# Attention in runs of a head pair, and its product with v by heads

## The chip, the cores and the metric

The kernel runs on one core of one Trainium2 chip. The metric is the device time of one execution in microseconds; the time before is the median of three runs. A profiled execution gives the trace from which all durations come.

## The reference

A two-layer encoder over 512 tokens of width 1024 (an 8 x 64 grid). Each layer is a half-step gated FFN, a mixer, and a second half-step FFN; the change lies in the attention of the mixer.

```
def mixer(h, w_in, gate_bias, rpb, w_na_out, w_f_out, w_o):
    z = h @ w_in                        # q, k, v (512 columns each), uf, ga, gf
    y_na = neighbourhood_attention(q, k, v, rpb) @ w_na_out
    y_f = fourier_mix(uf) @ w_f_out
    return (sigmoid(ga + gate_bias[0]) * y_na + sigmoid(gf + gate_bias[1]) * y_f) @ w_o

# attention, 8 heads of 64: blocks of 16 columns x 8 rows = 128 queries,
# each against a band of 32 columns x 8 rows = 256 keys
    s = einsum('brjqhd,brjuvhd->brjhquv', qg, k_win) * scale + bias      # masked to a 16-column window
    p = softmax(s)
    o = einsum('brjhquv,brjuvhd->brjqhd', p, v_win)
```

Everything is float32, and the kernel keeps that accuracy on TensorE by splitting each operand into a high part (rounded by ScalarE to the fp32r format) and a low part (the rest, by VectorE). A product is then three matmuls: high by high, high by low, low by high (`mm3`, lines 291 to 294).

## The kernel before, in words

Tokens are permuted so that 128 neighbouring positions are one block of queries j (0 to 3) and the 256 keys of a block are two consecutive pieces of 128 positions. The mixer (`stage_mixer`) first projects u and v with tokens on partitions: `proj_V` leaves four tiles of v (tag "v": high half, low half), and three DMA pairs build shifted tiles "vs" that straddle two of them, so that `vch` holds seven tiles of 128 keys. Then come the Fourier products (`four_pos`, `four_ch`) and, by head pair hp (heads 2hp and 2hp+1 on partitions 0 to 63 and 64 to 127), the projections of q and k with channels on partitions (`proj_q`, `proj_k`; 24 matmuls of 512 columns each, lines 292 to 294).

Attention goes in eight steps i = 2*hp + pr, each for one head pair and two query blocks. `att_step(i)` does three things one after the other: the product with v of step i-2 (`att_out`), the transposes of step i-1 (`att_trans`), and the scores and softmax of step i (`att_scores`):

- Scores: 12 matmuls with 64 rows each (line 1123), the two heads alternating on the two halves of the array, into two PSUM banks. VectorE adds bias and takes the maximum (line 1133), ScalarE does exp with the sum (1139) and scales by the reciprocal (1146).
- Transposes: 8 matmuls against the identity (line 1155) into two banks, each then split into the high and low part of a tile "p" (`split`, lines 298 and 299).
- Product with v: for each of two query blocks and two pieces of keys, `mm3` with v as the stationary operand (128 columns: both heads of the pair) and p as the moving one (256 columns: the queries of both heads). One PSUM bank holds the 128 x 512 result; of each 128 x 256 half only the quarters where the head of v meets its own queries are used. Lines 298 and 299 split these two pieces (64 partitions x 256) into "o".

A projection lies between the steps, and towards the end of the attention a fill: `f_fill` multiplies the Fourier result with its weights in eight parts of 12 matmuls (512 columns), which `next(f_fill)` places by hand between the steps. Behind the last step, `fill(o, ns, 0, w)` multiplies "o" with its weights, and the gate products follow.

Each engine works through its own instructions in the order that the scheduler of the framework set when the program was built: program order, unless an instruction is not ready and a later one is. `manual_schedule` blocks keep program order; weights are split two items ahead (`ws.prep`, lines 181 and 184; three buffers "whi", "wlo"). Buffers that matter: 8 PSUM banks; 23 buffers of 4 KB with the tag "k" (`slot`), for v, vs, y, q, k, p, o, fs, t1 and weights on their way; 8 of 2 KB (`tmp`).

Of the kernel before, what the change touches and what calls it, by code (L numbers as in the profile page):

```python
# [9 lines left out]
F32 = mybir.dt.float32  # L10
F32R = mybir.dt.float32r
BF16 = mybir.dt.bfloat16
I32 = mybir.dt.int32
AF = mybir.ActivationFunctionType
# [78 lines left out]
def encoder_kernel(  # L93
# [19 lines left out]
    def slot(dt=F32, s="k", shape=(4, 256)):  # L113
        return kp.tile([P, *shape], dt, tag="k", name=nm(s), bufs=23)

    def hilo(s):
        t = slot(F32R, s, (2, T))
        return t[:, 0, :], t[:, 1, :]

    def bank(s="ps"):  # L120
        return pp.tile([P, T], F32, tag="ps", name=nm(s))
# [133 lines left out]
    class Stream:  # L255
# [26 lines left out]
        def next(self):  # L282
            self.prep(self.pos + 1 + AHEAD)
            it = self.items[self.pos]
            self.pos += 1
            return it.out
# [4 lines left out]
    def mm3(ps, lh, ll, rh, rl, start, stop, again=False):  # L291
        PE.matmul(ps, lh, rh, start=start, stop=False, skip_group_check=again)  # L292
        PE.matmul(ps, lh, rl, start=False, stop=False, skip_group_check=again)  # L293
        PE.matmul(ps, ll, rh, start=False, stop=stop, skip_group_check=again)  # L294

    def split(hi, lo, src, scale=None):
        if scale is None:
            S.activation(hi, src, AF.Copy)
            V.tensor_tensor(lo, src, hi.bitcast(F32), ALU.subtract)
            return  # L300
        S.activation(hi, src, AF.Copy, scale=scale)
        V.scalar_tensor_tensor(lo, src, scale, hi.bitcast(F32), ALU.mult, ALU.subtract)
# [633 lines left out]
    def stage_mixer(l, norm, nxt):  # L936
        mp = mix_pool[0]

        def tmp(dt=F32, s="x"):
            return mp.tile([P, T], dt, tag="tmp", name=nm(s), bufs=8)  # L940
# [86 lines left out]
        def proj_V():  # L1027
            pss = [bank() for _ in range(4)]
            for g in range(4):
                for k, (wh, wl) in enumerate(wide()):  # L1030
                    kt = 2 * g + k
                    for c in range(4):
                        lh, ll = [z[:, c * P : (c + 1) * P] for z in xs[kt]]
                        mm3(pss[c], lh, ll, wh, wl, kt == 0, kt == DT - 1)
            outs = []
            for c in range(4):
                t = slot(F32R, "v", (2, T))
                split(t[:, 0, :], t[:, 1, :], pss[c], norm.r[:, c : c + 1])
                outs.append(t)
            return outs  # L1040

# [43 lines left out]
        def proj_q(hp):  # L1085
            q[hp] = proj_T(DH**-0.5)

        def proj_k(hp):
            k[hp] = proj_T(None)
            o.append(hilo("o"))  # L1090
# [19 lines left out]
                bms[hp].append(res)  # L1110

        def att_scores(i):
            hp, pr = divmod(i, 2)
            (qh, ql), (kh, kl) = q[hp], k[hp]
            ps = [bank(), bank()]
            for jj in range(2):
                j = 2 * pr + jj
                ks = slice(BAND[j] * 64, BAND[j] * 64 + 256)
                qs = slice(j * P, (j + 1) * P)
                for i, (a, b) in enumerate(((qh, kh), (qh, kl), (ql, kh))):  # L1120
                    for e in range(2):
                        r = slice(64 * e, 64 * e + 64)
                        PE.matmul(
                            ps[e][:, jj * 256 : (jj + 1) * 256], a[r, qs], b[r, ks], start=i == 0, stop=i == 2
                        )
            s_ = [tmp(s="s"), tmp(s="s")]
            nmx = sp.tile([P, 4], F32, tag="nmx", name=nm("nmx"), bufs=4)
            sm = sp.tile([P, 4], F32, tag="sm", name=nm("sm"), bufs=4)
            rs = sp.tile([P, 4], F32, tag="rs", name=nm("rs"), bufs=4)
            for e in range(2):  # L1130
                for jj in range(2):
                    c, z = slice(jj * 256, (jj + 1) * 256), 2 * e + jj
                    V.tensor_tensor_reduce(
                        s_[e][:, c], ps[e][:, c], bms[hp][e][:, pr + jj, :], -1.0, -NEG, ALU.add, ALU.min, nmx[:, z : z + 1]
                    )
            for e in range(2):
                for jj in range(2):
                    c, z = slice(jj * 256, (jj + 1) * 256), 2 * e + jj
                    S.activation(
                        s_[e][:, c], s_[e][:, c], AF.Exp, scale=-1.0, bias=nmx[:, z : z + 1], accum_out=sm[:, z : z + 1]  # L1140
                    )
                V.reciprocal(rs[:, 2 * e : 2 * e + 2], sm[:, 2 * e : 2 * e + 2])
            for e in range(2):
                for jj in range(2):
                    c, z = slice(jj * 256, (jj + 1) * 256), 2 * e + jj
                    S.activation(s_[e][:, c], s_[e][:, c], AF.Copy, scale=rs[:, z : z + 1])
            return s_

        def att_trans(s_):
            res = []  # L1150
            for jj in range(2):
                pt = bank()
                for e in range(2):
                    for c in range(2):
                        PE.transpose(
                            pt[:, (2 * c + e) * P : (2 * c + e + 1) * P],
                            s_[e][:, jj * 256 + c * P : jj * 256 + (c + 1) * P], ident,
                        )
                hi, lo = hilo("p")
                split(hi, lo, pt)  # L1160
                res.append((hi, lo))
            return res

        def att_out(i, p_):
            hp, pr = divmod(i, 2)
            po = bank()
            hs = slice(hp * P, (hp + 1) * P)
            for jj in range(2):
                ph, pl = p_[jj]
                for c in range(2):  # L1170
                    vh, vl = vch[BAND[2 * pr + jj] + 2 * c]
                    cs = slice(c * 256, (c + 1) * 256)
                    mm3(po[:, jj * 256 : jj * 256 + 256], vh[:, hs], vl[:, hs], ph[:, cs], pl[:, cs], c == 0, c == 1)
            pv = po.rearrange("p (a e q) -> p a e q", a=2, e=2)
            oh, ol = [z[:, pr * 256 : pr * 256 + 256].rearrange("p (a q) -> p a q", a=2) for z in o[hp]]
            for e in range(2):
                r = slice(64 * e, 64 * e + 64)
                split(oh[r], ol[r], pv[r, :, e, :])

        sc, pt_ = {}, {}  # L1180

        def att_step(i):
            if 0 <= i - 2 < 8:
                att_out(i - 2, pt_.pop(i - 2))
            if 0 <= i - 1 < 8:
                pt_[i - 1] = att_trans(sc.pop(i - 1))
            if i < 8:
                sc[i] = att_scores(i)


        def rows_of(src, tb, w):
# [11 lines left out]
        def fill(src, to, i, w=None):  # L1203

            w = w or [ws.next(), ws.next()]
            for tb in range(TB):
                if tb % 2 == 0:
                    to[i, tb // 2] = slot(F32, "fs", (2, T))
                ps = rows_of(src, tb, w)
                S.activation(to[i, tb // 2][:, tb % 2, :], ps, AF.Copy)  # L1210
                yield
# [94 lines left out]
        bias_for(0)  # L1306
        vs = []
        for s in range(3):
            t = slot(F32R, "vs", (2, T))
            nc.sync.dma_start(out=t[0:64].bitcast(F32), in_=vt[s][64:128].bitcast(F32))  # L1310
            nc.sync.dma_start(out=t[64:128].bitcast(F32), in_=vt[s + 1][0:64].bitcast(F32))
            vs.append(t)
        vch = {i: (t[:, 0, :], t[:, 1, :]) for i, t in ((0, vt[0]), (1, vs[0]), (2, vt[1]), (3, vs[1]), (4, vt[2]), (5, vs[2]), (6, vt[3]))}
        for g in range(4):
            four_pos(g)
        proj_q(0)
# [1 line left out]
        for g in range(4):  # L1318
            four_ch(g)
        proj_q(1)  # L1320
        for hp in range(3):
            bias_for(hp + 1)
            att_step(2 * hp)
            proj_k(hp + 1)
            att_step(2 * hp + 1)
            if hp < 2:
                proj_q(hp + 2)

        def f_rows():
            for i in range(2):  # L1330
                yield from fill(yf, fs, i)


        B = {(i, j): [z[i].bitcast(F32)[:, :, j * 256 : (j + 1) * 256] for z in (hx, lx)] for i in range(2) for j in range(2)}
# [7 lines left out]
            V.tensor_tensor(t[0], t[0], t[1], ALU.add)  # L1342
            yield t

        f_fill = f_rows()
        for i in range(6, 8):
            next(f_fill)
            next(f_fill)
            att_step(i)
        next(f_fill)  # L1350
        next(f_fill)
        first = minus(B[0, 0], B[0, 1], "t1")
        next(first)
        att_step(8)
        swap_pools(0)
        next(f_fill)
        next(first)
        att_step(9)
        t12, _ = next(first)
        ws.prep(ws.pos + 2)  # L1360
        next(f_fill)
        bias = []
        for which in range(2):
            b_ = slot(F32, "gb", (D,))
# [278 lines left out]
```

## Time and profile before

| | |
|---|---|
| time, median of 3 runs (lowest, highest) | 1911.06 us (1909.5, 1911.25) |
| the profiled execution: its time, its span | 1909.88 us, 1908.1 us |
| granted TensorE clock | 0.998 |
| busy: PE, DVE, ACT, POOL | 1894.6, 1609.9, 1162.8, 199.2 us |
| attention with its projections and fills | 406 to 482 us (layer 0), 1352 to 1429 us (layer 1) |

The page of the profile gives the busy time of each engine, the chain of work that ended last, and the costliest groups of instructions. The timeline lists instructions of one engine by start, duration, line, operation, tiles, shape and count; successive equal ones are merged, and the duration is then that of the whole row. Matmuls overlap: what one costs is the distance from its start to the next start. Windows give busy time of each engine in a stretch.

### The profile page before, as it was taken

Reading aid. Unit: us, or ns where it says so; the run is one execution under the profiler, and the core shown is the slowest. Engines: PE = TensorE matmul, PEld = TensorE weight load, DVE = VectorE, ACT = ScalarE, POOL = GpSimd, SP = SyncE. Lnnn points to the kernel's source line nnn. Section 1 sums busy time; section 2 is a strip of 40 time slices with the busy share of each in tenths; the row PEclk is TensorE's granted clock in tenths of the full one; section 3 lists DMA queues with packets and bytes.
Section 4 is the critical chain, followed back from the end, with each engine's and each line's share of the span. In section 5 each row is a group of like instructions: output and inputs, shape, how many; then the busy total and the mean of one; then the engine's idle time right before and its main releaser. Section 6 shows DMA issues by size and latency. Waiting matters only on the chain.

```text
span 1908.1 us, 25170 instructions
## 1 busy us (share of the span) xinstructions
PE 1894.6 (99%) x9189; PEld 1587.4 (83%) x9189; DVE 1609.9 (84%) x2000; ACT 1162.8 (61%) x1676; POOL 199.2 (10%) x246
## 2 busy tenths in 40 slices
PE   9999999999999999999999999999999999999998
PEld 7888888888888888888888888888888888888886
DVE  7877899586989987889997778995769899787898
ACT  6655665457666755566665556663675566555664
POOL 0101010300111010001010100103111101010010
PEclk9999999999999999999999999999999999999999
DMA  9776499321986777649877665974129867766594
GB/s 301 207 208 182 149 255 316 95 73 45 265 214 164 175 195 207 176 152 258 255 188 210 183 177 157 274 267 131 37 95 250 214 169 173 205 180 177 170 279 141
DMA packets 104924, 361.09 MB, mean 189 GB/s; under 512 B 12064, under 2 KB 14240, under 8 KB 104800
## 3 DMA queue, kind: packets, MB, share of 16 engines
q1 hardware_dynamic: 77856, 267.42, 39.9%
q0 software_dynamic: 26800, 92.04, 26.7%
q8 instruction: 72, 1.18, 0.2%
q14 instruction: 52, 0.43, 0.1%
q10 hardware_dynamic: 144, 0.02, 0.0%
HBM read 354.18 MB, written 2.11 MB: 187 GB/s over the span
## 4 chain that ended last, share of the span: by engine, by line
PE 98%; DVE 1%; DMA 1%; ACT 0%; issue 0%; DVEq 0%; ACTq 0%
PE A L453 9%; PE A L454 9%; PE A L456 9%; PE o L453 7%; PE o L454 7%; PE o L456 7%; PE ps L292 5%; PE ps L293 5%; PE ps L294 5%; PE B L453 5%; PE B L454 5%; PE B L456 5%; PE C L454 2%; PE C L453 2%; PE C L456 2%; PE tr L545 2%
## 5 line engine op out<-in xcount | busy, mean ns | idle before, releaser
L181 ACT ACTIVATE whi<-raw 128x1024 fp32r<-128x1024 f32 (+1 forms) x528 | 546.9, 1037 | 428.1 <-PE A L454 127.8
L184 DVE TENSOR_TENSOR wlo<-raw,whi 128x1024 fp32r<-128x1024 f32 (+1 forms) x528 | 629.0, 1196 | 195.7 <-ACT whi L181 194.3
L152 POOL DMA_DIRECT2D raw<-in_wst_dram x158 | 136.0, 870 | 1285.7 <-DMA raw<-in_wst_dram 574.5
L166 DVE TENSOR_TENSOR raw<-raw,raw 128x1024 f32<-128x1024 f32 (+1 forms) x146 | 172.2, 1189 | 1.2
L454 PE MATMUL A<-whi,xl 128*128 128x512 f32 x384 | 149.5, 389 | 0.0
L453 PE MATMUL A<-whi,xh 128*128 128x512 f32 x384 | 149.4, 389 | 0.0
L456 PE MATMUL A<-wlo,xh 128*128 128x512 f32 x384 | 110.5, 389 | 0.0
L176 ACT ACTIVATE whi<-raw 128x1024 fp32r<-128x1024 f32 (+1 forms) x79 | 81.8, 1035 | 41.5 <-PE A L454 12.5
L177 DVE SCALAR_TENSOR_TENSOR wlo<-raw,whi 128x1024 fp32r<-128x1024 f32 (+1 forms) x79 | 93.2, 1192 | 10.9 <-ACT whi L176 10.8
L638 ACT ACTIVATE th<-sn,rh 128x512 f32<-128x512 f32 x80 | 56.9, 714 | 69.0 <-DVE sn L527 69.0
L522 ACT ACTIVATE sn<-A 128x512 f32<-128x512 f32 x96 | 56.4, 589 | 49.4 <-PE A L456 49.4
L456 PEld LDWEIGHTS A<-wlo,xh 128*128 128x128 f32 x384 | 72.1, 188 | 15.0
L454 PEld LDWEIGHTS A<-whi,xl 128*128 128x128 f32 x384 | 72.1, 188 | 14.8
L453 PEld LDWEIGHTS A<-whi,xh 128*128 128x128 f32 x384 | 72.1, 188 | 14.8
L453 PE MATMUL B<-whi,t1h 128*128 128x512 f32 x192 | 76.2, 397 | 0.0
L453 PE MATMUL A<-whi,t3h 128*128 128x512 f32 x192 | 75.3, 392 | 0.0
L453 PE MATMUL C<-whi,xh 128*128 128x512 f32 x192 | 74.9, 390 | 0.0
L453 PE MATMUL A<-whi,t2h 128*128 128x512 f32 x192 | 74.9, 390 | 0.0
L454 PE MATMUL B<-whi,t1l 128*128 128x512 f32 x192 | 74.8, 390 | 0.0
L454 PE MATMUL A<-whi,t3l 128*128 128x512 f32 x192 | 74.8, 390 | 0.0
L454 PE MATMUL C<-whi,xl 128*128 128x512 f32 x192 | 74.7, 389 | 0.0
L454 PE MATMUL A<-whi,t2l 128*128 128x512 f32 x192 | 74.7, 389 | 0.0
(410 smaller groups left out, 4794.3 us busy)
## 6 DMA issues: line engine op xcount, KB each, us to landing
raw<-in_wst_dram SPq DMA_DIRECT2D x466, 512.0 KB
raw<-in_wst_dram POOLq DMA_DIRECT2D x162, 512.0 KB, 7.8
raw<-in_wst_dram SPq DMA_DIRECT2D x30, 256.0 KB
vs<-v SPq DMA_DIRECT2D x12, 256.0 KB
bw<-in_rpb_dram SPq DMA_DIRECT2D x32, 68.0 KB
x<-in_xin_dram SPq DMA_DIRECT2D x4, 512.0 KB
raw<-in_wst_dram POOLq DMA_DIRECT2D x8, 256.0 KB, 8.2
dft<-in_dft_dram POOLq DMA_DIRECT2D x8, 256.0 KB, 6.1
```

What stands on the lines that cost most here:

```text
L152: G.dma_start(out=self.t, in_=wst[GRAN_AT[self.plus]][:, 0 : self.n], accum_op=ALU.add)
L166: V.tensor_tensor(self.raw.t, self.raw.t, self.add.t, ALU.add)
L176: S.activation(hi, t, AF.Copy, scale=-1.0)
L177: self.last = V.scalar_tensor_tensor(lo, t, -1.0, hi.bitcast(F32), ALU.mult, ALU.subtract)
L181: S.activation(hi[:, cs], t[:, cs], AF.Copy)
L184: self.last = V.tensor_tensor(lo[:, cs], t[:, cs], hi[:, cs].bitcast(F32), ALU.subtract)
L292: PE.matmul(ps, lh, rh, start=start, stop=False, skip_group_check=again)
L293: PE.matmul(ps, lh, rl, start=False, stop=False, skip_group_check=again)
L294: PE.matmul(ps, ll, rh, start=False, stop=stop, skip_group_check=again)
L453: PE.matmul(ps, lh, rh, start=start, stop=False, skip_group_check=again)
L454: PE.matmul(ps, ll, rh, start=False, stop=False, skip_group_check=again)
L456: PE.matmul(ps, lh, rl, start=False, stop=stop, skip_group_check=again)
```

## The change

`proj_V` writes v in another layout: for each head pair four groups of 64 columns, namely high part of the first head, its low part, low part of the second head, its high part. So 128 successive columns hold both parts of one head.

Scores, transposes and products are made for a whole head pair at a time: `att_next(hp)` transposes both steps of pair hp-1 and makes the scores of both steps of pair hp in one run, then the softmax of both; `att_outs(hp)` makes both products with v in one run, behind the next `proj_k` or behind fills. The hand-written order of fills and steps is changed with it.

The product with v goes by heads: the stationary operand is the 128 columns (high and low part of v) of one head, the moving one is 256 columns (high and low part of p for that head's 128 queries). One matmul gives all four products of parts. Each head has a bank of its own. Three of the four quarters are summed outside: ScalarE copies low v by high p to the other half of the partitions, VectorE adds high by high and high by low, and the sum ("ot", both heads) is split into the high and low part of "o".

```diff
--- before.py
+++ after.py
@@ -1034,8 +1034,15 @@
                         mm3(pss[c], lh, ll, wh, wl, kt == 0, kt == DT - 1)
             outs = []
             for c in range(4):
-                t = slot(F32R, "v", (2, T))
-                split(t[:, 0, :], t[:, 1, :], pss[c], norm.r[:, c : c + 1])
+
+                t = slot(F32R, "v", (D,))
+                v_ = t.rearrange("p (h s d) -> p h s d", s=4, d=DH)
+                ps = pss[c].rearrange("p (h e d) -> p h e d", e=2, d=DH)
+                r = norm.r[:, c : c + 1]
+                S.activation(v_[:, :, 0::3, :], ps, AF.Copy, scale=r)
+                for e in range(2):
+                    hi, lo = v_[:, :, 3 * e, :], v_[:, :, 1 + e, :]
+                    V.scalar_tensor_tensor(lo, ps[:, :, e, :], r, hi.bitcast(F32), ALU.mult, ALU.subtract)
                 outs.append(t)
             return outs
 
@@ -1110,6 +1117,7 @@
                 bms[hp].append(res)
 
         def att_scores(i):
+
             hp, pr = divmod(i, 2)
             (qh, ql), (kh, kl) = q[hp], k[hp]
             ps = [bank(), bank()]
@@ -1123,6 +1131,10 @@
                         PE.matmul(
                             ps[e][:, jj * 256 : (jj + 1) * 256], a[r, qs], b[r, ks], start=i == 0, stop=i == 2
                         )
+            return ps
+
+        def att_probs(i, ps):
+            hp, pr = divmod(i, 2)
             s_ = [tmp(s="s"), tmp(s="s")]
             nmx = sp.tile([P, 4], F32, tag="nmx", name=nm("nmx"), bufs=4)
             sm = sp.tile([P, 4], F32, tag="sm", name=nm("sm"), bufs=4)
@@ -1156,36 +1168,47 @@
                             pt[:, (2 * c + e) * P : (2 * c + e + 1) * P],
                             s_[e][:, jj * 256 + c * P : jj * 256 + (c + 1) * P], ident,
                         )
-                hi, lo = hilo("p")
-                split(hi, lo, pt)
-                res.append((hi, lo))
+                p2 = slot(F32R, "p", (2, T))
+                split(p2[:, 0, :], p2[:, 1, :], pt)
+                res.append(p2)
             return res
 
         def att_out(i, p_):
             hp, pr = divmod(i, 2)
-            po = bank()
-            hs = slice(hp * P, (hp + 1) * P)
-            for jj in range(2):
-                ph, pl = p_[jj]
-                for c in range(2):
-                    vh, vl = vch[BAND[2 * pr + jj] + 2 * c]
-                    cs = slice(c * 256, (c + 1) * 256)
-                    mm3(po[:, jj * 256 : jj * 256 + 256], vh[:, hs], vl[:, hs], ph[:, cs], pl[:, cs], c == 0, c == 1)
-            pv = po.rearrange("p (a e q) -> p a e q", a=2, e=2)
-            oh, ol = [z[:, pr * 256 : pr * 256 + 256].rearrange("p (a q) -> p a q", a=2) for z in o[hp]]
+            t = tmp(s="ot")[:, 0:256] if i < 6 else slot(F32, "ot", (D,))[:, 0:256]
             for e in range(2):
-                r = slice(64 * e, 64 * e + 64)
-                split(oh[r], ol[r], pv[r, :, e, :])
+
+                po = bank()
+                hs = slice((2 * hp + e) * P, (2 * hp + e + 1) * P)
+                for jj in range(2):
+                    for c in range(2):
+                        v_ = vch[BAND[2 * pr + jj] + 2 * c][:, hs]
+                        z = slice((2 * c + e) * P, (2 * c + e + 1) * P)
+                        PE.matmul(po[:, jj * 256 : jj * 256 + 256], v_, p_[jj][:, :, z], start=c == 0, stop=c == 1)
+                pv = po.rearrange("p (a s q) -> p a s q", a=2, s=2)
+                r, x_ = slice(DH * e, DH * e + DH), slice(DH - DH * e, 2 * DH - DH * e)
+                to = t[r].rearrange("p (a q) -> p a q", a=2)
+                S.activation(to, pv[x_, :, 0, :], AF.Copy)
+                for s_ in range(2):
+                    V.tensor_tensor(to, pv[r, :, s_, :], to, ALU.add)
+            oh, ol = [z[:, pr * 256 : pr * 256 + 256] for z in o[hp]]
+            split(oh, ol, t)
 
         sc, pt_ = {}, {}
 
-        def att_step(i):
-            if 0 <= i - 2 < 8:
-                att_out(i - 2, pt_.pop(i - 2))
-            if 0 <= i - 1 < 8:
-                pt_[i - 1] = att_trans(sc.pop(i - 1))
-            if i < 8:
-                sc[i] = att_scores(i)
+        def att_outs(hp):
+            for i in (2 * hp, 2 * hp + 1):
+                att_out(i, pt_.pop(i))
+
+        def att_next(hp):
+
+            if hp:
+                for i in (2 * hp - 2, 2 * hp - 1):
+                    pt_[i] = att_trans(sc.pop(i))
+            if hp < 4:
+                ps = [att_scores(i) for i in (2 * hp, 2 * hp + 1)]
+                for i, p in zip((2 * hp, 2 * hp + 1), ps):
+                    sc[i] = att_probs(i, p)
 
 
         def rows_of(src, tb, w):
@@ -1306,11 +1329,11 @@
         bias_for(0)
         vs = []
         for s in range(3):
-            t = slot(F32R, "vs", (2, T))
+            t = slot(F32R, "vs", (D,))
             nc.sync.dma_start(out=t[0:64].bitcast(F32), in_=vt[s][64:128].bitcast(F32))
             nc.sync.dma_start(out=t[64:128].bitcast(F32), in_=vt[s + 1][0:64].bitcast(F32))
             vs.append(t)
-        vch = {i: (t[:, 0, :], t[:, 1, :]) for i, t in ((0, vt[0]), (1, vs[0]), (2, vt[1]), (3, vs[1]), (4, vt[2]), (5, vs[2]), (6, vt[3]))}
+        vch = {i: t for i, t in ((0, vt[0]), (1, vs[0]), (2, vt[1]), (3, vs[1]), (4, vt[2]), (5, vs[2]), (6, vt[3]))}
         for g in range(4):
             four_pos(g)
         proj_q(0)
@@ -1318,17 +1341,25 @@
         for g in range(4):
             four_ch(g)
         proj_q(1)
-        for hp in range(3):
-            bias_for(hp + 1)
-            att_step(2 * hp)
-            proj_k(hp + 1)
-            att_step(2 * hp + 1)
-            if hp < 2:
-                proj_q(hp + 2)
-
         def f_rows():
             for i in range(2):
                 yield from fill(yf, fs, i)
+
+        f_fill = f_rows()
+
+        def f_some(n):
+            for _ in range(n):
+                next(f_fill)
+
+        for hp in range(3):
+            att_next(hp)
+            bias_for(hp + 1)
+            proj_k(hp + 1)
+            if hp:
+                att_outs(hp - 1)
+            if hp < 2:
+                proj_q(hp + 2)
+        f_some(2)
 
 
         B = {(i, j): [z[i].bitcast(F32)[:, :, j * 256 : (j + 1) * 256] for z in (hx, lx)] for i in range(2) for j in range(2)}
@@ -1342,23 +1373,20 @@
             V.tensor_tensor(t[0], t[0], t[1], ALU.add)
             yield t
 
-        f_fill = f_rows()
-        for i in range(6, 8):
-            next(f_fill)
-            next(f_fill)
-            att_step(i)
-        next(f_fill)
-        next(f_fill)
+        att_next(3)
+        f_some(2)
+        att_outs(2)
+        f_some(1)
         first = minus(B[0, 0], B[0, 1], "t1")
         next(first)
-        att_step(8)
+        next(first)
+        att_next(4)
         swap_pools(0)
-        next(f_fill)
-        next(first)
-        att_step(9)
+        f_some(1)
+        att_outs(3)
         t12, _ = next(first)
         ws.prep(ws.pos + 2)
-        next(f_fill)
+        f_some(2)
         bias = []
         for which in range(2):
             b_ = slot(F32, "gb", (D,))
```

## The prediction

> **What bounds the kernel now.** I read the page first: busy times, then the chain.
>
> ```profile
> span 1908.1 us, 25170 instructions
> ...
> PE 1894.6 (99%) x9189; PEld 1587.4 (83%) x9189; DVE 1609.9 (84%) x2000; ACT 1162.8 (61%) x1676; POOL 199.2 (10%) x246
> ...
> PE 98%; DVE 1%; DMA 1%; ACT 0%; issue 0%; DVEq 0%; ACTq 0%
> ```
>
> TensorE sets the end: 98% of the chain is its matmuls. So matmul time taken out anywhere shortens the kernel, as long as nobody comes late. Next I asked for the timeline of PE in the attention of layer 0, one step from transposes to transposes.
>
> ```profile
> 421.84 1.04 PE L1155 MATMUL ps<-ident,s 128*128 128x128 f32 x8
> 422.80 0.97 PE L1123 MATMUL ps<-q,q 64*128 64x256 f32 x12
> 423.70 0.50 PE L292 MATMUL ps<-xh,whi 128*128 128x512 f32 x1
> 424.05 0.40 PE L293 MATMUL ps<-xl,whi 128*128 128x512 f32 x1
> ...
> 429.32 0.28 PE L292 MATMUL ps<-p,vs 128*128 128x256 f32 x1
> 429.43 0.28 PE L293 MATMUL ps<-p,vs 128*128 128x256 f32 x1
> ...
> 430.75 1.04 PE L1155 MATMUL ps<-ident,s 128*128 128x128 f32 x8
> ```
>
> A step lasts 430.75 - 421.84 = 8.91 us without a gap. Its parts by distance of starts: 24 projection matmuls at 0.227 (5.44), 12 products at 0.12 (1.43), 8 transposes at 0.109 (0.87), six pairs of scores at 0.115 (0.69). That makes 8.43. The other 0.47 us belongs to the score run: its first pair starts 0.20 after the last transpose and the second 0.22 after the first; the projection starts 0.20 after the last pair, and its second matmul 0.34 later instead of 0.227. Every run of 64-row matmuls pays this once, however long it is.
>
> Then the windows of the two steps of a head pair, for the cover that the other engines have (columns: PE, PEld, DVE, ACT, POOL busy us).
>
> ```profile
> 423.00:432.00 9.00, 9.00 (x60) 7.69 (x60) 6.30 (x18) 6.76 (x20) 0.00 (x0) 1.00 0.10 20
> 432.00:441.00 9.00, 9.00 (x62) 7.69 (x62) 6.30 (x18) 6.90 (x19) 4.10 (x6) 1.00 0.00 0
> ```
>
> Per 9 us, DVE has 2.7 us to spare and ACT 2.1 to 2.2. Last, ACT and DVE in order of time.
>
> ```profile
> 422.91 0.36 ACT L298 ACTIVATE o<-ps 64x256 fp32r<-64x256 f32 x1
> 423.17 1.06 ACT L298 ACTIVATE p<-ps 128x512 fp32r<-128x512 f32 x2
> 426.82 0.51 ACT L1139 ACTIVATE s<-s,nmx 128x256 f32<-128x256 f32 x1 [1.74 <-DVE nmx L1133]
> 428.81 1.70 ACT L1146 ACTIVATE s<-s,rs 128x256 f32<-128x256 f32 x4
> ...
> 424.26 0.41 DVE L299 TENSOR_TENSOR o<-ps,o 64x256 fp32r<-64x256 f32 x1
> 426.37 0.41 DVE L1133 CUSTOM_DVE_ANT_0 s<-ps,bm 128x256 f32<-128x256 f32 x1
> ```
>
> Softmax of a step fills ACT from 426.82 to 430.51 (3.69), and the transposes that need it start at 430.75: the margin is only 0.25 us, so covers matter here.
>
> **The change, part by part.**
>
> Products with v: 8 matmuls of 256 columns where there were 12. 4 x 0.12 = 0.48 us less in each of 8 steps x 2 layers: 7.7 us, on PE, hence on the path. The two pieces of the moving operand lie apart; the trace has no such row, and I take the 0.12 of the contiguous row (bounds: 0.11, as the narrower transposes, and 0.18, which would eat the gain).
>
> Scores: four runs per layer instead of eight, 8 fewer in all. At 0.47 each: 3.8 us (at least 0.40, by the four distances alone: 3.2). Transposes in longer runs gain nothing: 8 of them and a following 512-column matmul are as long as alone (475.32 to 476.43).
>
> Together PE loses 11.5 us. A pair's two steps last 16.4 instead of 17.8.
>
> Added on ACT: the copy takes the place of the old high part (64x256, 0.36). New is one split of 128x256 per step; the nearest row is L1146 with 0.40 to 0.49. 16 times: 6.4 to 7.8 us. Added on DVE: per step four additions and one low part where two low parts were, three more instructions of 0.34 to 0.43 (the L299 row on "o"), 48 in all: 16 to 21 us. Cover per pair: DVE had 5.4 to spare, loses 1.43 by the shorter round and 2.4 (at 0.40) by the additions, and keeps 1.6; ACT had 4.3, loses 1.43 and 0.9, and keeps 2.0. So I cost them at nothing in the sum; without that cover they are rival B.
>
> V's layout: 4 low parts of 0.75 become 8 of 128x256 (0.42 by the L1057 row, 0.34 between starts), per layer 0 to +0.4 us on DVE. It delays the low parts of the Fourier tiles, the last of which ends at 395.83; its product comes near 399.5. Nothing. The shifted-copy DMAs keep their size. The bias issues on SP (4 per pair) and their POOL additions move behind the scores; nothing on POOL or SP waits for the scores but the mask sums' buffers, and they are needed a round (16 us) later. Nothing.
>
> What comes late instead. Three places, per layer:
>
> 1. In the rounds. With both steps' softmax in one block (2 x 3.69 = 7.4 us on ACT), the low parts of p (4 x 0.65 on DVE) before it, and between scores and transposes 5.44 + 1.92 + 5.44 = 12.8 us of PE work, about 2 us are left. But the new sums hold four PSUM banks until ACT is through with the softmax. I take 0.3 us for a bank that is late (0 to 1.5).
>
> 2. At the end. Between the last scores and the last transposes lie two fill parts, the products of pair 2 and one fill part: 5.44 + 1.92 + 2.72 = 10.1 us. Counted from the first transpose of pair 2: scores end at 1.74 + 1.85 = 3.6, the first maximum waits for p's low parts until 4.0, softmax runs from 4.4 to 11.8, a weight split (1.05) and two fill copies (2 x 0.5) have to be put in, 13.8; the transposes are due at 13.7. I take 0.7 (0 to 2.3, all of these ahead of it plus one 1.05 split).
>
> 3. Buffers with the tag "k". When the last transposes are split, 7 tiles of v, 4 of y, 4 of o, 3 of fs, 2 of t1 and 4 of p want 24 of 23. Before, out(6) gave its two p back before those of step 7 were written; now both steps are transposed first, so the last p waits for the products of step 6 and is needed 0.36 us behind them. Its way is shown by
>
> ```profile
> 475.95 0.60 ACT L298 ACTIVATE p<-ps 128x512 fp32r<-128x512 f32 x1
> 476.58 0.69 DVE L299 TENSOR_TENSOR p<-ps,p 128x512 fp32r<-128x512 f32 x1 [0.24 <-ACT p L298]
> ```
>
> 0.28 (end of the last product) + 0.04 + 0.63 + 0.69 + 0.07 - 0.36 = 1.35 us of stall in PE's queue, with products and fills behind it. Bounds: 0 if the scheduler lets the next fill go first, and 3.6 if a weight split (1.05 on ACT, 1.2 on DVE) is ahead.
>
> The fills behind that (5.44 us plus the first 2.04 of the next product) cover the sums of pair 3, about 4 to 7 us: nothing.
>
> Sum: 1909.9 - 11.5 + 2 x (0.3 + 0.7 + 1.35) = 1903.1 for the profiled execution. That one lies 1.2 below the median, so 1904.3 in the median. With all three at their ends: 1898.4 to 1913.2, or 1899.6 to 1914.4 in the median.
>
> **Rivals.**
>
> A, the whole gain: the scheduler fills every wait with ready fills. 1909.9 - 11.5 + 1.2 = 1899.6. For it: PE waits nowhere in the attention before, although margins are 0.25 us. Against it: 24 of 23 buffers.
>
> B, slower: ACT and DVE take turns instead of overlapping. While ACT does 7.4 us of softmax, the copies of the products queue behind it on ACT, so the additions can't start; DVE has only its own remaining maxima (2.3) and one projection (0.69) and idles 4.4 us. A round is then DVE's 12.6 + 2.4 + 4.4 = 19.4 instead of 17.8, +1.6 in three rounds of each layer; the first round keeps its 1.43. 1909.9 + 9.6 - 2.9 + 1.2 = 1917.8. It decides from 1.4 us of idle DVE per round (PE begins to wait) and loses from 2.8 on. For it: DVE would be at 15.0 of 16.4. Against it: the order on ACT before was "o, p, p, o" where the program has "o, o, p, p", so the scheduler does fill gaps, and DVE's 12.6 include waits. [...]
>
> C, the runs are broken up: projections slip in between the scores, and only the products gain. 1909.9 - 7.7 + 4.7 + 1.2 = 1908.1.
>
> D, between: the three stalls at their upper ends (7.4 per layer) give the gain back, 1914.4; half way there 1909.4.
>
> [...]
>
> **How the numbers follow.** Forecast 0.42, with an own range of 1900.5 to 1907; A 0.18; C 0.07; D 0.15; B 0.18. About 0.2% (3.8 us) is what a measurement of this kernel can tell from no change. Faster: forecast and A, 0.60. Same (1907.2 to 1914.9): C and D, 0.22. Slower: B, 0.18. The range from 1898.5 to 1915 leaves out B and a little below A, 2 in 10.
>
> **What would show it.** Scores in rows of 24, products of 8 at 0.12; PE's busy time down by about 11 us; DVE's up by 16 to 21 and ACT's by 6 to 8. Stalls: PE waiting for "p" before the last product, and for "s" or a bank before the last transposes, about 1 us each. I am wrong if products are spaced over 0.15, if a score run costs the same per 12, or if PE waits in each round for the softmax or for the additions.

## The result, and the profile after

The changed kernel takes 1918.53 us (median of 6 runs, 1916.71 to 1920.01) where the kernel before takes 1910.99 on the same chip: a ratio of 1.0038, 95% interval 1.0027 to 1.0049. It is slower by 7.5 us; predicted was 1904.3, with a range that ended at 1915.0. Rival B (1917.8, with a chance of 0.18) came nearest.

The page of the changed kernel:

```profile
span 1917.5 us, 25147 instructions
...
PE 1891.5 (99%) x9125; PEld 1583.7 (83%) x9125; DVE 1629.4 (85%) x2056; ACT 1168.7 (61%) x1692; POOL 199.0 (10%) x246
...
PE 89%; DVE 4%; ACT 3%; issue 2%; DMA 1%; SPq 0%; POOL 0%; DVEq 0%; POOLq 0%; ACTq 0%
```

The work is what was forecast: DVE has 19.5 us more (16 to 21 expected), ACT 5.9 (6.4 to 7.8 expected), and TensorE 64 matmuls fewer. But the chain, 98% TensorE before, now runs 7% through DVE and ACT, and PE's busy time fell by 3.1 us instead of 11.

The timeline of PE in the attention of layer 0 (start, duration of the row, what, count, and in brackets the wait ahead of it):

```profile
406.20 1.69 PE L1131 MATMUL ps<-q,q 64*128 64x256 f32 x24
...
418.84 1.91 PE L1167 MATMUL ps<-ident,s 128*128 128x128 f32 x16
...
428.35 0.40 PE L1187 MATMUL ps<-p,v 128*128 128x256 f32 x2
428.58 0.40 PE L1187 MATMUL ps<-p,vs 128*128 128x256 f32 x2
...
437.57 1.08 PE L1131 MATMUL ps<-q,q 64*128 64x256 f32 x13
439.70 0.98 PE L1131 MATMUL ps<-q,q 64*128 64x256 f32 x11 [1.04 <-DVE q L977]
442.03 0.50 PE L292 MATMUL ps<-xh,whi 128*128 128x512 f32 x1 [1.36 <-DVE p L299]
...
465.66 0.40 PE L1187 MATMUL ps<-p,v 128*128 128x256 f32 x2
...
473.12 0.63 PE L1167 MATMUL ps<-ident,s 128*128 128x128 f32 x4 [1.20 <-DVE ot L1193]
...
479.20 0.74 PE L1187 MATMUL ps<-p,v 128*128 128x256 f32 x4 [2.64 <-DVE p L299]
```

The first rows show the change at work: scores in a run of 24, transposes in one of 16, and products two by two at 0.12 us each ((428.58 - 428.35) / 2). The rows with brackets are new. The waits of PE over the whole kernel (total, times, longest) show the same places in both layers:

```profile
PE ps L1187 <- DVE p L299: 5.3, 2, 2.6
PE ps L292 <- DVE p L299: 4.0, 5, 1.4
PE ps L138 <- ACT warm L135: 2.7, 1, 2.7
PE ps L1167 <- DVE ot L1193: 2.4, 2, 1.2
PE ps L1131 <- DVE q L977: 2.1, 2, 1.1
```

All but the third, which is the start-up and stood there before, end with DVE: 13.8 us. So who makes DVE late? ACT and then DVE at the end of pair 2, in order of time:

```profile
468.55 1.70 ACT L1158 ACTIVATE s<-s,rs 128x256 f32<-128x256 f32 x4
470.15 1.06 ACT L1233 ACTIVATE fs<-ps 128x512 f32<-128x512 f32 x2
471.24 1.59 ACT L1191 ACTIVATE ot<-ps 64x256 f32<-64x256 f32 x4
```

```profile
466.31 1.23 DVE L184 TENSOR_TENSOR wlo<-raw,whi 128x1024 fp32r<-128x1024 f32 x1 [1.66 <-ACT whi L181]
467.69 0.17 DVE L1154 RECIPROCAL rs<-sm 128x2 f32<-128x2 f32 x1 [0.16 <-ACT s L1151]
468.68 0.17 DVE L1154 RECIPROCAL rs<-sm 128x2 f32<-128x2 f32 x1 [0.82 <-ACT s L1151]
471.65 2.69 DVE L1193 TENSOR_TENSOR ot<-ps,ot 64x256 f32<-64x256 f32 x6 [2.80 <-ACT ot L1191]
...
475.73 1.23 DVE L1371 TENSOR_TENSOR t<-xh 128x1024 f32<-128x1024 f32 x1
...
477.21 1.22 DVE L1371 TENSOR_TENSOR t<-xl 128x1024 f32<-128x1024 f32 x1
478.45 2.48 DVE L299 TENSOR_TENSOR p<-ps,p 128x512 fp32r<-128x512 f32 x4
```

TensorE does the products of pair 2 from 465.66 on and is through with them before 468, yet ACT copies them only at 471.24, behind the whole softmax of pair 3 and two copies of the fill. Until then DVE idles 1.66 + 0.16 + 0.82 + 2.80 = 5.4 us; the first 1.66 lies ahead of the first finished product, so some 3.8 us are what earlier copies could have used. Afterwards everything falls due at once: eight additions, two subtractions for the gates, and only then the low parts of p, for which TensorE waits 2.64 us.

The last piece was not in the prediction. Windows of the changed kernel, in two pairs (columns: PE, PEld, DVE, ACT, POOL busy, then the granted TensorE clock):

```profile
439.27:442.68 3.41, 1.63 (x14) 1.33 (x15) 3.41 (x6) 2.58 (x5) 0.00 (x0) 1.00 0.00 0
442.68:446.10 3.42, 3.42 (x10) 2.67 (x9) 3.42 (x16) 1.90 (x8) 0.00 (x0) 0.50 0.00 0
476.83:480.25 3.42, 1.05 (x7) 0.99 (x8) 3.39 (x6) 2.32 (x5) 0.90 (x1) 1.00 0.54 153
480.25:483.66 3.41, 3.41 (x15) 3.09 (x14) 3.29 (x7) 2.71 (x6) 0.87 (x1) 0.50 0.95 298
```

Behind both of these bunches of waits the granted clock is 0.50 for 3.41 us; matmuls of 512 columns come every 0.43 us instead of 0.227. Ahead of the last 3.7 us of the span, which are at 0.50 too, there are four such stretches, 13.65 us, two of them in a row in layer 1; the kernel before is at 0.50 in the last 6.4 us of its span alone.

### The profile page after: what moved, and what is told of

Read it like the earlier page. It is cut to its first block, busy times and chain, and to the rows that moved or that the text cites. A ratio compares the mean times of both kernels' runs of the same rounds, so it can differ in the third digit from the quotient of the medians.

```text
span 1917.5 us, 25147 instructions
## 1 busy us (share of the span) xinstructions
PE 1891.5 (99%) x9125; PEld 1583.7 (83%) x9125; DVE 1629.4 (85%) x2056; ACT 1168.7 (61%) x1692; POOL 199.0 (10%) x246
## 4 chain that ended last, share of the span: by engine, by line
PE 89%; DVE 4%; ACT 3%; issue 2%; DMA 1%; SPq 0%; POOL 0%; DVEq 0%; POOLq 0%; ACTq 0%
PE A L453 9%; PE A L454 9%; PE A L456 9%; PE o L453 7%; PE o L454 7%; PE o L456 7%; PE B L453 4%; PE B L454 4%; PE B L456 4%; PE ps L292 3%; PE ps L294 3%; PE ps L293 3%; PE C L454 2%; PE C L453 2%; PE C L456 2%; PE tr L545 2%
```

## The experiments

Theory 1 (order): the pair's softmax, one block of 7.4 us on ACT, holds back the copies of the products, so DVE idles and is late afterwards. Theory 2 (amount): DVE has too much to do, in any order. Theory 3 (holding): the longer runs hold PSUM banks and buffers for longer, whatever the product. The kernel before ran beside each group, at 1910.1 to 1911.1, so kernels of different groups can be compared to about 1 us.

The attention of layer 0, from its first score matmul to the first product of the gates, read from each timeline, goes with the whole time. The profiled executions of e12 and e4 were their slowest (1908.2 and 1918.18): e12's attention takes 85.72 in layer 1, 1.60 less than in layer 0; e4's granted clock is 0.996, where the changed kernel has 0.995 and the kernel before 0.998.

| kernel | attention, us | time, us (lowest to highest) | ratio to before, 95% |
|---|---|---|---|
| before | 87.81 | 1910.99 | |
| changed | 93.09 | 1918.53 (1916.71 to 1920.01) | 1.0027 to 1.0049 |
| e1 products by heads only | 90.50 | 1914.42 (1912.77 to 1917.64) | 1.0009 to 1.0028 |
| e2 runs only | 86.30 | 1907.53 (1906.23 to 1910.24) | 0.9974 to 0.9992 |
| e3 copies and additions first | 84.51 | 1902.14 (1902.06 to 1902.69) | 0.9938 to 0.9968 |
| e12 copies first | 87.32 | 1904.49 (1904.16 to 1908.2) | 0.9959 to 0.9982 |
| e5 no additions | 84.65 | 1904.15 (1902.08 to 1905.42) | 0.9947 to 0.9977 |
| e9 as e3, no additions | 85.37 | 1904.8 (1903.25 to 1905.49) | 0.9955 to 0.998 |
| e11 as e1, maxima first | 88.39 | 1910.07 (1909.0 to 1911.79) | 0.9988 to 1.0006 |
| e4 one subtraction later | 92.40 | 1915.17 (1913.65 to 1918.18) | 1.0014 to 1.0032 |
| e7 TensorE kept busy | 91.07 | 1918.03 (1916.63 to 1920.28) | 1.0025 to 1.005 |

**e2 and e1: each part of the change alone.** e2 keeps the changed order of runs, with the old product (`mm3`) and layout of v. e1 keeps the steps of before, with the product by heads.

> The runs of a head pair alone, with the old product (three matmuls, two splits of 64x256 per step, no additions). T1: the splits of o queue behind the softmax on ACT too, but DVE has 3 instructions less per step behind them: some stalls, 1908 to 1913. T2: none, 3.8 less than before: 1906 to 1908. T3: the stalls of the changed kernel but for the products' gain: 1918 to 1926.

> The product by heads alone, in the old steps (one step's softmax at a time). Theory T1 (the pair's softmax in one block of 7.4 us on ACT holds back the copies, DVE idles and then comes late): the block is 3.7 us here, so hardly a stall; 128 products less at 0.12 us, 7.7 less than before, at most 2 given back: 1903 to 1906, no slow-clock stretch. Theory T2 (the 48 additional DVE instructions, 20 us, are simply too much for the attention in any order): DVE is late in each step, 1912 to 1920. Theory T3 (it is the runs themselves, through banks and buffers held longer): 1903.

The runs bring 3.5 us, where 3.8 were predicted, with one wait of 0.39 in each layer; so longer runs by themselves hold up next to nothing, and theory 3 falls. The products by heads, which should bring 7.7 (64 matmuls fewer at 0.12; the 128 in the text above is a slip), lose 3.4. Both times lie in theory 2's ranges, not in theory 1's; e3 and e12 have to decide. Waits of PE in e1:

```profile
PE ps L1182 <- DVE p L299: 3.2, 2, 1.6
PE ps L1162 <- ACT s L1153: 2.9, 8, 0.4
...
PE ps L293 <- DVE wlo L184: 2.7, 2, 1.3
```

So the loss comes with the sum outside, and it needs no block of two softmaxes: in single steps too, additions and low parts of o stand on DVE ahead of what the next softmax needs (0.36 us late, eight times). Theory 1 in its narrow form missed here.

**e3: the copies and additions get the first place in their queues.** The scheduler then takes them as soon as they are ready; the work is the same.

```diff
-                S.activation(to, pv[x_, :, 0, :], AF.Copy)
-                for s_ in range(2):
-                    V.tensor_tensor(to, pv[r, :, s_, :], to, ALU.add)
+                with tc.high_priority():
+                    S.activation(to, pv[x_, :, 0, :], AF.Copy)
+                    for s_ in range(2):
+                        V.tensor_tensor(to, pv[r, :, s_, :], to, ALU.add)
```

> The changed kernel with the copies and additions of the product given priority, so that ACT does them between the instructions of the second softmax. Same work. T1: DVE works in the time it idled in, the stalls of pair 2 (2.4 us per layer) and the bank wait (1.2) go and with them most of the slow clock: 1904 to 1909. T2: nothing changes by more than 2: 1916 to 1920. T3: banks are freed earlier, so 1908 to 1914.

1902.14: 16.4 us less than the changed kernel, 8.9 below the kernel before, and below the ranges of all three theories; theory 1's, from 1904 on, is the nearest. Page, DVE's timeline at the same place, and PE's waits of e3:

```profile
PE 1883.7 (99%) x9125; PEld 1578.7 (83%) x9125; DVE 1627.6 (86%) x2056; ACT 1168.6 (61%) x1692; POOL 199.6 (11%) x246
```

```profile
464.38 3.47 DVE L1194 TENSOR_TENSOR ot<-ps,ot 64x256 f32<-64x256 f32 x8
...
468.67 1.22 DVE L1372 TENSOR_TENSOR t<-xh 128x1024 f32<-128x1024 f32 x1
469.81 1.22 DVE L1372 TENSOR_TENSOR t<-xl 128x1024 f32<-128x1024 f32 x1
471.05 2.48 DVE L299 TENSOR_TENSOR p<-ps,p 128x512 fp32r<-128x512 f32 x4
```

```profile
PE ps L1167 <- ACT s L1158: 2.7, 2, 1.3
PE ps L292 <- DVE p L299: 1.6, 4, 0.4
```

PE's first product of pair 2 is at 461.50 here. The additions begin 2.9 us behind it (464.38), where the changed kernel took 6.0 (465.66 to 471.65), and the low parts of p 9.6 us behind it (471.05) in place of 12.8. No product with v waits for p any more, and the granted clock is 0.998, as before the change (0.995 in the changed kernel). DVE's busy time is within 1.8 us of the changed kernel's: theory 2 falls.

**e12: the copies alone get the first place** (the additions stay outside the `with`), to tell ACT's queue from DVE's.

> The changed kernel (1918.5) with only ACT's copies of the products given the first place, the additions on DVE left in their old place. The copies are what the late end is put down to: ACT does them behind a pair's whole softmax, while DVE stands idle. If that is so, moving the copies alone brings most of the 16.4 us that moving copies and additions brought: 1902 to 1907. If DVE's own order (additions ahead of the low parts of q and p) is what counts, it stays at 1913 to 1918.

ACT at the end of pair 2:

```profile
464.80 0.38 ACT L1192 ACTIVATE ot<-ps 64x256 f32<-64x256 f32 x1
465.08 0.50 ACT L1158 ACTIVATE s<-s,rs 128x256 f32<-128x256 f32 x1
465.60 0.78 ACT L1192 ACTIVATE ot<-ps 64x256 f32<-64x256 f32 x2
466.29 0.50 ACT L1158 ACTIVATE s<-s,rs 128x256 f32<-128x256 f32 x1
466.81 0.38 ACT L1192 ACTIVATE ot<-ps 64x256 f32<-64x256 f32 x1
```

1904.49: 14.0 of the 16.4 us come with four 0.4 us copies per pair going between softmax instructions instead of behind them. DVE keeps its order, additions ahead of subtractions and low parts of p; only the additions begin sooner, 465.53 - 406.48 = 59.1 us after the first scores in place of 471.65 - 406.20 = 65.5. One wait of 1.2 us per layer for p stays at the last products.

**e5 and e9: the additions left out,** in the changed kernel and in e3. One copy of the high by high part stands for each sum of three.

> The changed kernel without the additions: ACT copies high by high only and DVE adds nothing, so two of the three products of parts are left out of the sum (64 DVE instructions of 0.43 us, some 28 us of DVE). Matmuls are all there. T1: copies are as late as before, but DVE has 1.7 us less per step behind them; stalls shrink to 1 to 3 us per layer: 1901 to 1907. T2: all stalls go: 1899 to 1901. T3: banks and buffers as before: 1914 to 1918.

> The kernel with the copies and additions of the products given the first place in their queues (1902.1), with the additions left out: one copy takes one of the three parts of each product's sum, and two are left out. It gives what the 16 to 21 us of additions on DVE cost once the order is right. If they are hidden then, as the prediction had it for the whole change, 1900.5 to 1903. If their amount alone costs: 1896 to 1899.

In the changed order the additions cost 14.4 us, as theory 1 expected; in the order of e3 leaving them out gains nothing: e9 is slower than e3 by 2.7, above both expected ranges. With the 28 us gone from DVE the scheduler placed the rest in another order, and the products wait for p again (1.2 us per layer), behind the two subtractions. An engine's amount and its order are two different things.

**e4: one subtraction behind the last transposes,** where the kernel before had it.

```diff
         next(first)
-        next(first)
         att_next(4)
         swap_pools(0)
+        next(first)
```

> The changed kernel (1918.5), with only the second of the two 1.2 us subtractions (t1) traced behind the last transposes, as in the kernel before, so that it no longer lies ahead of the last low parts of p on DVE. If the late end of the pair is a matter of what stands on DVE between the late additions and the low parts, the last wait of 2.64 us shortens by about 1.2 per layer: 1914 to 1916.5, and 1911 to 1913 if the half-clock stretches near 480 and 1429 to 1436 go with it. If the wait comes from the copies alone, whatever stands behind them, it stays within 1 us of 1918.5.

The wait at the last products fell from 2.64 to 1.6, by 1.0 where 1.2 was expected, and the time by 3.4. The 1.6 that are left end with ACT's copy of a fill, no longer with DVE. So here what stands behind a late copy on DVE added to the stall. In the profiled execution the granted clock is 0.996 (0.995 in the changed kernel, 0.998 before), so stretches at half clock are left; which of them, is not shown.

**e7: TensorE kept busy during the last wait,** by 9 matmuls per layer.

```diff
                 po = bank()
+                if i == 6 and e == 0:
+                    for _ in range(9):
+                        PE.matmul(po, vch[0][:, 0:P], vch[0][:, 0:T], start=True, stop=True)
```

> The changed kernel (1918.5) with 9 further matmuls of 128x512 (0.227 us each at full clock, 2.04 us) per layer, whose results nothing reads, put on TensorE ahead of the products of pair 3, where it waits 2.64 us for p; no other engine has more or less to do. If an idle TensorE is what halves its clock, the half-clock stretches at 480 and at 1429 to 1436 go, and with them up to 1.7 us for each of the three: 1913.5 to 1917. If the clock falls for another cause, they stay: 1918 to 1920. If the matmuls don't fit into the wait, up to 4 us come on top.

```profile
476.83:480.25 3.42, 2.83 (x18) 2.22 (x17) 3.36 (x7) 2.20 (x6) 0.90 (x1) 1.00 0.91 302
480.25:483.66 3.41, 3.41 (x18) 2.88 (x18) 3.25 (x7) 2.39 (x5) 0.87 (x1) 1.00 1.01 244
```

The half-clock stretches at the ends went (from 1425.74 to 1432.56 the clock is 1.00 as well), with nothing changed but TensorE's idleness. The one at 442.68 went too (1.00 from 424 to 464), although the edit leaves its waits (1.06 and 1.36) as they were, and a new one came at 1392.25, behind the same two waits in layer 1 (clock 0.96 from 1374 to 1394 and from 1394 to 1414): whether these waits are followed by half clock differs from execution to execution. The price can be read once cleanly: from the first scores to the products of pair 1 the changed kernel takes 449.24 - 406.20 = 43.04 us, e7 41.41, with the same waits; that is 1.63 for one stretch. The attentions became shorter by 2.0 and 1.35 us. In layer 0, 1.63 of the 2.0 are the stretch at 442.68, so the end gained only 0.4, or 0.9 if a wait of 0.5 that is new there is added. The span became shorter by 1.5 (1917.5 to 1916.0), with 1.6 us of waits in the FFNs, and the median can't be told from the changed kernel's. My 1913.5 to 1917 missed: 1918.03 lies in the range for another cause. The windows speak for idleness as the cause, the time doesn't show it, and a stretch at the end of a layer cost less than 1.63 here.

**e11: the order on DVE in single steps.** e1, with the scores' maxima first on DVE.

> The kernel of before's steps with the products by heads (1914.4), with the scores' maxima on DVE (four of 0.35 us per step) given the first place in its queue, so that the four additions and the low parts of o (some 3 us per step) stand behind them. There each step's transposes waited 0.36 us for the softmax, whose first instruction stood behind additions. If it is the order on DVE and not the amount of additions that cost this form its gain, the waits of the softmax (2.9 us) go: 1908 to 1912, and towards the 1903 of the prediction's minus 7.7 if the waits of p go as well. If the amount costs: 1913 to 1917.

1910.07: 4.3 of e1's loss come back, so the order on DVE is part of it there as well. The waits for s fell from 2.9 to 1.3 us, they did not go; with those for p and wlo 5.7 us stay, and why these do I did not separate.

**On from e3.** Its largest wait left is that of the last transposes for the softmax, 1.33 us per layer. Four tries: e8 puts one more part of the fill (12 matmuls, 2.7 us; the text below has twice that) ahead of these transposes; e6 takes e4's edit too; e10 traces the splits of o later; e13 gives the softmax's reciprocals the first place as well.

> The kernel with copies and additions first (1902.1), with one more part of f's fill (24 matmuls, some 5.4 us) put ahead of the last transposes, and one less behind the last products. Its largest wait left is 1.33 us per layer of these transposes for the softmax; that goes: 1899.5 to 1900.5, if nothing later than it waits. If the end of the layer's attention is set by the last products' additions and splits, the part missing behind them costs as much or more: 1902 to 1906.

> The kernel with copies and additions first (1902.1), with the second t1 subtraction traced behind the last transposes as well. In that kernel the products of pair 3 didn't wait for p, so the subtraction lies in idle time of DVE and nothing is to be gained: 1901 to 1903. If the last softmax steps, for which the transposes wait 1.33 us per layer, come earlier for it, 1899.5 to 1900.5; if the subtraction is late for the gates, 1903 to 1905.

> The kernel with copies and additions first (1902.1), with the splits of the attention's result o traced behind the next transposes or the next q. In that kernel two of them (0.42 us each, and 0.36 of waiting for an addition) stood on ACT ahead of the last softmax steps, for which the transposes waited 1.33 us per layer. If that place is the cause, 1.0 to 1.3 us per layer go: 1899.5 to 1900.5. If the fill's copies on ACT (1.09 us) hold the softmax back all the same, or a later wait takes its place, 1901.5 to 1904.

> The kernel with copies and additions first (1902.1), with the softmax's reciprocals on DVE (0.09 us each) given the same first place, so that by their earlier place in the program they go ahead of the eight additions. In that kernel the last two softmax steps on ACT came behind a reciprocal that DVE did at 467.88, behind 3.47 us of additions, and the transposes waited 1.33 us per layer for them. If that is the place, 1.0 to 1.3 us per layer go: 1899.5 to 1900.3, and the waits for s vanish. If ACT's other work (fill copies, splits of o) is what holds the softmax back, they stay: 1901.5 to 1903.5.

e8: 1902.97 (0.9949 to 0.9974); that wait went, and 0.8 us for o and two waits of 1.2 and 1.1 inside the gate products (e3 has one of 0.6) took its place. e6: 1903.12 (0.9952 to 0.9977), 0.1 above the range for no gain. e10: 1910.41 (0.9992 to 1.0009), outside both expectations: the wait stayed at 1.4, and another of 1.6 us came at the fill of o, whose weight split now stood on ACT behind a fill's copy that itself waited for TensorE. e13: 1904.5 (0.9963 to 0.9982), above both ranges; waits of PE:

```profile
PE ps L292 <- DVE p L299: 2.9, 4, 1.1
...
PE ps L1188 <- DVE p L299: 1.5, 2, 0.7
PE ps L1168 <- DVE ot L1195: 0.6, 2, 0.3
```

The wait for s is gone, so the cause was the reciprocal, 0.1 us of work behind 3.47 us of additions. But the last low parts of p moved back by 1.0 us against the start of the attention (472.38 - 406.36, against 471.05 - 406.05), and the round's wait for them grew from 0.4 to 1.1. None of the four beats e3.

## Why the prediction was wrong, point by point

**Right: what TensorE saves.** Products at 0.12, a score run cheaper by 0.47: e3's PE is busy 10.9 us less than before (11.5 predicted), and e2 confirms the runs by themselves. The two pieces of the moving operand cost nothing: 0.12 us per product, as before. e3 also checks the sum: 87.81 less 5.75 (half of 11.5) is 82.06; its waits of 0.4, 0.4 and 1.33 make it 84.2, and 84.51 was measured.

**Right: the added amounts** on DVE and ACT, within the bounds or half a microsecond under.

**Wrong: "So I cost them at nothing in the sum".** This is the step that failed. The cover of 1.6 us per pair on DVE was a balance of busy times over a round. It counted idle time that DVE could not use, because each addition waits for a copy on ACT, and the copy's place in ACT's queue was behind 7.4 us of softmax. e12 shows it: with only the copies moved, the kernel with the same additions is 14.0 us faster.

**Wrong: the three stalls.** In place of 0.3, 0.7 and 1.35 stood, per layer, 2.8 in the rounds (0.39, 1.04, 1.36), 1.20 at the last transposes and 2.64 at the last products: 6.6, not 2.35, the first of them over its upper bound of 1.5. The causes differed as well. The last transposes waited for a bank that an addition had to release, not for the softmax. The last products waited for the first low part of p, which stood with the other three behind the additions and subtractions on DVE. The 24 of 23 buffers did not come into it, for ACT wrote the high parts of all four p in one row, over at 479.15, before the first of these products began at 479.20:

```profile
477.09 2.06 ACT L298 ACTIVATE p<-ps 128x512 fp32r<-128x512 f32 x4
```

**Missing: the clock.** Behind waits this close together TensorE's clock was halved, at 1.6 us a stretch where that could be read. Layer 0 of the changed kernel adds up to 82.06 + 6.63 of waits + 2 x 1.7 (half of each 3.41) = 92.1, of 93.09 measured; at least 1.0 us is not accounted for.

**Rival B had the mechanism.** It named the copies behind the softmax and 4.4 us of idle DVE (5.4 measured, 3.8 of it with products to copy), far over its deciding 1.4; its 1917.8 is 0.7 from the result. That it came so near is in part luck: it expected 1.6 us in each of three rounds and nothing for the end or the clock, while most was lost there. The argument against it, that the scheduler does fill gaps, was read from single steps, where copies and softmax had not been traced as blocks; the scheduler did not put the copies between the softmax instructions until it was told to. That argument cost B the chance it deserved. In e1 the products alone turned an expected saving of 7.7 us into a loss of 3.4; e3, with the same work 8.9 us below the kernel before, shows that it was the order in which the banks of the products are emptied, not the amount of that work.

## What to carry to other kernels

When a sum moves from TensorE to two other engines in a chain (copy on one, addition on the other), don't set busy time against spare time: follow the first link's place in its queue, ask what block it stands behind, and what else falls due when it is released. Long blocks of one kind made fewer switches on TensorE here (0.47 us for each score run saved) and longer queues elsewhere (the copies behind 7.4 us of a pair's softmax); short instructions that release another engine should go between them. Giving them the first place brought 16.4 us with the same instructions, but every further reordering only moved the wait, so measure each.

## What the hardware showed that was not expected

In the changed kernel, 1.8 us of idleness within 3.41 were followed by half clock on TensorE. The stretches at 0.50 start at 442.70, 480.25 and 1429.15 us and last 3.41, 3.41 and 6.83 us; their starts are 37.55 and 948.90 us apart, which is 11 and 278 times 3.413. On this grid the windows ahead of them had PE busy for 1.63, 1.05 (both shown above) and 1.41 of 3.41 us (the last ahead of the two in a row), so 1.8 to 2.4 us idle stood ahead of each. It went with where the waits fell: the waits of 1.04 and 1.36 us in layer 0 put 1.8 us of idleness into one window, and a half-clock stretch followed; in layer 1 a boundary of the grid fell between the same two, 1.06 us idle from 1388.19 to 1391.60 and 1.36 from there to 1395.02, and the clock stayed at 1.00 until 1414.

The limit stays open. In e10, by the distances of matmul starts, TensorE was idle for 1.79 us ahead of 482.04, and from 483.65 on starts came 0.43 us apart; in layer 1 it waited as long at this place (3.3 us for the two waits), and the attention took 87.02 us against 88.68 in layer 0, 1.66 less, so by its length none followed there. In e12, where the attention of layer 0 is 1.60 longer than that of layer 1, about the price of one stretch, the longest wait of TensorE behind the start-up is 1.2 us. Where the traces show both sides, in the changed kernel, e7 and e10, each stretch seen in the attention stands behind 1.8 us of idleness or more within 3.41 (2.0 in e7, 0.6 and 1.36 ahead of 1392.25), or behind another stretch, which speaks for idleness as the cause; what else decides is not shown.
